# First norm and first projections of a two-layer decoder in an order written out for four engines, with identity turns ahead of the data

## The chip, the cores and the metric

The kernel runs on one core of a Trainium2 chip. The metric is the time of one execution on the device in microseconds (us), and the time given is the median of the runs. The core has TensorE (PE; its weight loads, PEld, are listed apart), VectorE (DVE), ScalarE (ACT), GpSimd (POOL) and the queue of SyncE (SPq), from which all transfers of this kernel are issued. TensorE writes its results into PSUM, eight banks of 512 fp32 columns, and reads both operands from SBUF.

## The reference

The kernel computes a two-layer decoder trunk over 1024 tokens of width 1024, in fp32. Only the beginning of the first layer matters here:

```python
def rms_norm(x, g):
    y = x * lax.rsqrt(jnp.mean(x * x, axis=-1, keepdims=True) + EPS)
    return y * g

def mla_swa_layer(x, positions, g_in, w_in, g_q_a, w_q_up, g_kv_a, w_kv_up, sinks, w_out):
    h = rms_norm(x, g_in)
    z = h @ w_in
    cq, ckv, kpe, q_s, k_s, v_s, gate = split_cols(z, EVEN_SPLITS)   # 256, 128, 32, 512, 128, 128, ...
    q = rms_norm(cq, g_q_a) @ w_q_up
    kv = rms_norm(ckv, g_kv_a) @ w_kv_up
    ...  # rotary on parts of q and on kpe, latent attention, window attention, gate, output projection
```

The second layer (forgetting attention) and the final norm follow.

## The kernel before

Every fp32 product is made of three matmuls: both operands are split into a rounded high part and a low part (high x high, low x high, high x low; `mm3`, lines 114 to 116). So each weight and each activation that TensorE reads has first been cast on ScalarE (the high part) and subtracted on VectorE or GpSimd (the low part): `split` (L105 and L106) for tiles that come out of PSUM, `split_sb` (L110 and L111) for weights in SBUF.

The tokens are 8 blocks of 128, handled as two halves of four blocks. For the first norm, each block's 1024 values are squared and summed (`square_sum`, L143 on VectorE, L146 on ScalarE), `inv_rms` (L118 to L139) makes 1/sqrt by a starting guess and three rounds of Newton's method on VectorE, and the row is multiplied by it (`row_norm`, L560 to L574, which deals the rows out to engines). `norm_T` (L200) then turns the half chunk by chunk: for each of the 8 chunks of 128 features, four 128x128 transposes into one PSUM bank (L206) and a split with the gain, which gives `hh` and `hl`.

The projections of a block of tokens (`token_project`) keep the activations stationary and stream the weights: 24 matmuls of 256 columns per block for the query latent (`za`, banks `pj`), 24 matmuls of 288 columns for the key/value latent, the rope key and the window values (`zb`, banks `s`). Each block has its own accumulator, filled over all 8 chunks before the next block begins. Then the latents are normed, turned and split again (`cT`), tables of cosines and sines are turned (`csE`, `csO`, L726 to L736), the rope keys are made (`krs`), the window keys are projected (`swa_k`), and the up-projections (`up_q`, `up_k`, `up_v`) begin.

A planner puts the instructions of each engine into an order by its own simulated times; the program text gives only the priorities. `tc.issue_after(ins)` keeps a group behind an instruction of the same engine, and inside `tc.manual_schedule(engines=...)` the named engines take their instructions in the order of the text. In the kernel before, only TensorE's order in the two attention parts is written out that way. The weights come through four buffers of 2 KB (`wr`), so a weight transfer waits until an older piece has been split.

Of the kernel before, what the change touches and what calls it, by code (L numbers as in the profile page):

```python
# [12 lines left out]
F32R = mybir.dt.float32r  # L13
# [5 lines left out]
P = 128  # L19
# [31 lines left out]
WORK0 = "q1 g0 q2 s0 q3 s1 s2 s3 a1 p0 b1 p1 g2 p2 g3 p3"  # L51
W_START0 = "FFFLLFLFLF"
# [7 lines left out]
def trunk(ctx, tc, x, positions, e_g_in, e_w_in, e_g_q_a, e_w_q_up, e_g_kv_a, e_w_kv_up,  # L60
# [13 lines left out]
            "wr": (4, 2048), "wh": (3, 2048), "wl": (3, 2048),  # L74
# [43 lines left out]
    def inv_rms(ssq, n, width, more=None):  # L118
# [13 lines left out]
        for _ in range(3):  # L132
            if n == 1:
                nc.vector.scalar_tensor_tensor(out=t, in0=y, scalar=y, in1=h, op0=ALU.mult, op1=ALU.mult)
            else:
                nc.vector.tensor_tensor(out=t, in0=y, in1=y, op=ALU.mult)
                nc.vector.tensor_tensor(out=t, in0=t, in1=h, op=ALU.mult)
            nc.vector.scalar_tensor_tensor(out=y, in0=t, scalar=1.5, in1=y, op0=ALU.add, op1=ALU.mult)
# [27 lines left out]
    def token_weights(pieces, cuts, tags_h, tags_l):  # L166

        n = sum(b - a for _, a, b in pieces)
        parts = []
        for (k0, kn), th, tl in zip(cuts, tags_h, tags_l):  # L170
# [7 lines left out]
            parts += [(wh[:, k, :], wl[:, k, :]) for k in range(kn)]  # L178
        return parts, n
# [20 lines left out]
    def norm_T(blocks, hT, gcol):  # L200

        hh, hl = hT
# [5 lines left out]
        return last  # L208
# [327 lines left out]
    nc.vector.tensor_copy(out=post, in_=p_ps[:, 0:NB])  # L536
    cost, sint = sbt("og", [NB, 16]), sbt("og", [NB, 16])
# [22 lines left out]
    def row_norm(rows, vector, groups, engines):  # L560
        ssq = sbt("sm", [4])
        for b in range(4):
            square_sum(rows[b], ssq[:, b:b + 1], vector[b] == "V")
        for a, n in groups:
            y = inv_rms(ssq[:, a:a + n], n, D)
            for b in range(a, a + n):
                yb = y[:, b - a:b - a + 1]
                if engines[b] == "A":
                    nc.scalar.activation(out=rows[b], in_=rows[b], func=AF.Copy, scale=yb)
                elif engines[b] == "P":  # L570
                    normalise(rows[b], yb, 1.0)
                else:
                    last = nc.vector.tensor_scalar(out=rows[b], in0=rows[b], scalar1=yb, scalar2=None, op0=ALU.mult)
        return last.ins  # L574
# [30 lines left out]
    g_ps = pst("pj", 32)  # L605
    nc.tensor.transpose(out=g_ps[:, 0:19], in_=gst[0:19], identity=ident[0:19, 0:19])
    gains = cp.tile([P, 19], F32, name="gains")
    nc.vector.tensor_copy(out=gains, in_=g_ps[:, 0:19])
# [13 lines left out]
    hT = []  # L622
    for hf in range(2):
        rows = xrows[4 * hf:4 * hf + 4]
        if hf:
            with tc.issue_after(normed):
                normed = row_norm(rows, "AAAV", [(0, 1), (1, 3)], "PVVA")
        hT.append(new_hT())
        made = norm_T([lambda k, r=r: r[:, k * P:(k + 1) * P] for r in rows], hT[hf], 0)

    with tc.issue_after(normed):
# [4 lines left out]
    with tc.issue_after(made):  # L636
        nc.vector.tensor_scalar(out=nsinks, in0=sinks, scalar1=-1.0, scalar2=None, op0=ALU.mult)


    zb, _ = token_weights([(w0, 256, 416), (w0, VS, VS + 128)], [(0, 3), (3, 3), (6, 2)],  # L640
                          ["kh", "kh", "kx"], ["kl", "kl", "kx"])
    kpe = sbt("gt", [NB, 32])
    cqs, ssq_q, ssq_kv = [], [], []
    for hf in range(2):
        cq, ssq = sbt("r1", [4, 256]), sbt("sm", [4])
        for b in range(4):
            acc = pst("pj", 256)
            token_project(hf * 4 + b, hT, za, acc)
            nc.vector.tensor_copy(out=cq[:, b, :], in_=acc)
            square_sum(cq[:, b, :], ssq[:, b:b + 1])  # L650
        cqs.append(cq)
        ssq_q.append(ssq)
# [24 lines left out]

    cT = [(sbt("qh", [S], F32R), sbt("ql", [S], F32R)) for _ in range(2)]
    for hf in range(2):
        y = inv_rms(ssq_q[hf], 4, 256)  # L680
        for b in range(4):
            nc.vector.tensor_scalar(out=cqs[hf][:, b, :], in0=cqs[hf][:, b, :], scalar1=y[:, b:b + 1],
                                    scalar2=None, op0=ALU.mult)
        for c in range(2):
            t = pst("t")
            for b in range(4):
                nc.tensor.transpose(out=t[:, b * P:(b + 1) * P], in_=cqs[hf][:, b, c * P:(c + 1) * P],
                                    identity=ident)
            cols = slice(hf * 512, (hf + 1) * 512)
            split(cT[c][0][:, cols], cT[c][1][:, cols], t, gains[:, 16 + c:17 + c])  # L690
    ckv = sbt("r1", [NB, P])
    for hf in range(2):
        ssq = sbt("sm", [4])
        for b in range(4):
# [99 lines left out]
    for _ in swa_k():  # L794
        pass
# [447 lines left out]
```

## Time and profile before

| what | us |
|---|---|
| median of 3 runs (1208.22 to 1209.9) | 1209.25 |
| profiled execution | 1211.98 |
| its span, first to last instruction | 1209.8 |
| TensorE busy in the span | 1164.8 (96%) |
| VectorE busy | 736.1 (61%) |
| ScalarE busy | 712.1 (59%) |
| GpSimd busy | 606.6 (50%) |

Times inside the kernel are counted from the start of the span. A busy time counts an engine's instructions from start to end. Matmuls are pipelined, so the step from one start to the next tells more of TensorE's speed than a duration does. The column for the granted TensorE clock is 1.00 in every stretch listed here.

### The profile page before, as it was taken

How to read it: one execution, taken by the hardware profiler on the slowest of the kernel's cores; microseconds unless marked ns; L12 is line 12 of the kernel's file. 1: busy time of each engine (PE TensorE's matmuls, PEld its weight loads, DVE VectorE, ACT ScalarE, POOL GpSimd, SP SyncE). 2: the span in 40 equal slices, each digit the busy share in tenths (PEclk: the TensorE clock that was granted, in tenths of full speed). 3: DMA queues.
4: the chain of work that ended last, by engine and by line, in shares of the span. 5: the costliest groups of instructions: out<-in, count | busy, mean ns of one | idle time of the engine just before them, and what ended most of it. 6: DMA issues, size and time to landing. Idle time of an engine off the chain costs nothing. (4 is left out here: it accounts for less than half of the span.)

```text
span 1209.8 us, 20486 instructions
## 1 busy us (share of the span) xinstructions
PE 1164.8 (96%) x6746; PEld 1010.1 (83%) x6746; DVE 736.1 (61%) x1962; ACT 712.1 (59%) x1599; POOL 606.6 (50%) x753
## 2 busy tenths in 40 slices
PE   4999999999898989999999999999999999999997
PEld 4997788888887878889998888888888888878886
DVE  8954466677676776665003666666656666657754
ACT  5634477776676765664214666676767666756442
POOL 6501144564765666433204555556565555568552
PEclk9999999999999999999999999999999999999999
DMA  6316412443755544563313221313131223236541
GB/s 213 91 43 231 152 45 69 119 139 103 204 149 144 166 139 153 171 212 105 114 44 107 62 79 58 92 53 88 53 94 62 83 69 102 65 122 212 185 161 61
DMA packets 171168, 139.52 MB, mean 115 GB/s; under 512 B 54027, under 2 KB 140838, under 8 KB 171062
## 3 DMA queue, kind: packets, MB, share of 16 engines
q1 hardware_dynamic: 171062, 138.21, 38.0%
q8 instruction: 53, 0.87, 0.3%
q14 instruction: 53, 0.43, 0.1%
HBM read 100.62 MB, written 37.55 MB: 114 GB/s over the span
## 5 line engine op out<-in xcount | busy, mean ns | idle before, releaser
L114 PE MATMUL pj<-hh,wh 128*128 128x512 f32 (+1 forms) x792 | 320.8, 405 | 2.2 <-ACT wh L110 0.9
L116 PE MATMUL pj<-hh,wl 128*128 128x512 f32 (+1 forms) x792 | 309.3, 391 | 0.6 <-POOL wl L111 0.6
L115 PE MATMUL pj<-hl,wh 128*128 128x512 f32 (+1 forms) x792 | 308.9, 390 | 0.0
L111 POOL TENSOR_TENSOR wl<-wr,wh 128x512 fp32r<-128x512 f32 (+1 forms) x146 | 183.8, 1261 | 161.6 <-ACT wh L110 153.4
L103 DVE TENSOR_TENSOR pl<-t,ph 128x512 fp32r<-128x512 f32 (+1 forms) x320 | 178.8, 563 | 86.6 <-ACT ph L102 84.3
L276 POOL TENSOR_SCALAR r<-r,sm 128x128 f32<-128x128 f32 (+4 forms) x248 | 167.1, 682 | 106.9 <-DVE sm L323 60.0
L102 ACT CAST ph<-t 128x512 fp32r<-128x512 f32 (+1 forms) x320 | 153.5, 483 | 106.4 <-PE t L347 86.0
L116 PEld LDWEIGHTS pj<-hh,wl 128*128 128x128 f32 x792 | 148.8, 188 | 33.5 <-POOL wl L111 1.1
L321 ACT ACTIVATE r<-r,sm 128x128 f32<-128x128 f32 (+7 forms) x184 | 143.0, 777 | 53.7 <-DVE sm L314 52.0
L114 PEld LDWEIGHTS pj<-hh,wh 128*128 128x128 f32 x792 | 149.3, 189 | 24.7 <-ACT wh L110 1.3
L115 PEld LDWEIGHTS pj<-hl,wh 128*128 128x128 f32 x792 | 149.6, 189 | 20.3
L347 PE MATMUL t<-ident,r 128*128 128x128 f32 x828 | 137.5, 275 | 11.6 <-DVE pl L103 9.1
L347 PEld LDWEIGHTS t<-ident,r 128*128 128x128 f32 x828 | 102.8, 141 | 40.0 <-DVE pl L103 11.2
L110 ACT CAST wh<-wr 128x512 fp32r<-128x512 f32 (+1 forms) x146 | 87.5, 600 | 58.1 <-PE pj L115 24.4
L308 POOL TENSOR_TENSOR ld<-ld,zrow 128x128 f32<-128x128 f32 x128 | 58.7, 468 | 99.7 <-DVE sm L314 80.2
L338 PE MATMUL o<-ph,v 128*128 128x512 f32 (+3 forms) x288 | 106.9, 371 | 0.0
L314 DVE CUSTOM_DVE_ANT_0 r<-s,ld 128x512 f32<-128x512 f32 (+1 forms) x120 | 70.5, 588 | 50.2 <-PE s L261 45.9
L339 PE MATMUL o<-pl,v 128*128 128x512 f32 (+3 forms) x288 | 99.4, 346 | 0.0
L285 POOL TENSOR_TENSOR v<-ge,v 128x512 fp32r<-128x512 f32 x26 | 34.6, 1330 | 71.1 <-ACT v L284 71.1
L338 PEld LDWEIGHTS o<-ph,v 128*128 128x128 f32 x288 | 54.9, 191 | 7.0
L339 PEld LDWEIGHTS o<-pl,v 128*128 128x128 f32 x288 | 54.6, 190 | 5.7
L114 PE MATMUL pj<-qh,hh 128*128 128x256 f32 (+1 forms) x176 | 50.9, 290 | 3.2 <-DVE gt L1057 1.7
(324 smaller groups left out, 2516.0 us busy)
## 6 DMA issues: line engine op xcount, KB each, us to landing
wr<-in_o_w_in SPq DMA_DIRECT2D x62, 256.0 KB, 3.1
wr<-ogs SPq DMA_DIRECT2D x44, 256.0 KB, 3.8
ld<-lcs SPq DMA_DIRECT2D x16, 512.0 KB, 4.1
ogs<-og SPq DMA_DIRECT2D x28, 256.0 KB, 2.0
ge<-vscr SPq DMA_DIRECT2D x24, 256.0 KB, 3.8
gt<-x1s SPq DMA_DIRECT2D x23, 256.0 KB, 2.9
wr<-ogs SPq DMA_DIRECT2D x24, 192.0 KB, 3.0
wr<-in_e_w_in SPq DMA_DIRECT2D x16, 256.0 KB, 3.3
```

Of the source, the lines that this page charges most:

```text
L102: nc.scalar.copy(out=hi, in_=src)
L103: nc.vector.tensor_tensor(out=lo, in0=src, in1=hi.bitcast(F32), op=ALU.subtract)
L110: nc.scalar.copy(out=hi, in_=raw)
L111: (engine or nc.gpsimd).tensor_tensor(out=lo, in0=raw, in1=hi.bitcast(F32), op=ALU.subtract)
L114: nc.tensor.matmul(out=o, lhsT=ah, rhs=bh, start=first, stop=False)
L115: nc.tensor.matmul(out=o, lhsT=ah, rhs=bl, start=False, stop=False)
L116: nc.tensor.matmul(out=o, lhsT=al, rhs=bh, start=False, stop=last)
L276: nc.gpsimd.tensor_scalar(out=row, in0=row, scalar1=rc, scalar2=scale, op0=ALU.mult, op1=ALU.mult)
L321: nc.scalar.activation(out=row[:, 0:L], in_=row[:, 0:L], func=AF.Exp, scale=-1.0, bias=mn, accum_out=den)
L338: nc.tensor.matmul(out=O[0][:, cols], lhsT=v()[:, j, :], rhs=ph[:, cols], start=j == 0, stop=False)
L339: nc.tensor.matmul(out=O[0][:, cols], lhsT=v()[:, j, :], rhs=pl[:, cols], start=False, stop=j == n - 1)
L347: nc.tensor.transpose(out=t[:, b * P:(b + 1) * P], in_=rows[b][:, j * P:(j + 1) * P], identity=ident)
```

## The change

Nothing is computed differently but for the form of three rounds in `inv_rms`. What moves or is added:

- 58 transposes of the identity into a bank that is not read (`WARM`), on TensorE ahead of the first data.
- For one value per partition, `inv_rms` uses `tensor_scalar` with two scalar operands in place of `scalar_tensor_tensor`.
- `wr` has six buffers; the first four weight pieces are loaded by name (`za_raw`).
- The first half's rows are squared, scaled and multiplied in a written order on four engines: row 0 squared on VectorE and rows 1 to 3 on ScalarE, one scale chain per row (`row_scales`), the products on GpSimd but for half of row 3.
- The query latent of a half is accumulated chunk by chunk in four banks at once (`latent_q`: two `pj`, two `o`): per chunk, twelve matmuls over the four blocks, two chunks behind the turns.
- Between these chunks the second half's rows are squared, at the seventh chunk their four scales are made together and the products written, and after it the second weight set is split.
- TensorE then takes, in a written order, the second half's turns between the first half's key/value blocks, the second half's query latent, and the other key/value blocks with the turns of the latents and the window keys among them.
- The rotary angles and the sinks' sign are issued behind the last split of the second half.

```diff
+WARM = 58
-            "wr": (4, 2048), ...
+            "wr": (6, 2048), ...
             if n == 1:
-                nc.vector.scalar_tensor_tensor(out=t, in0=y, scalar=y, in1=h, op0=ALU.mult, op1=ALU.mult)
...
+                nc.vector.tensor_scalar(out=t, in0=y, scalar1=y, scalar2=h, op0=ALU.mult, op1=ALU.mult)
+                nc.vector.tensor_scalar(out=y, in0=t, scalar1=1.5, scalar2=y, op0=ALU.add, op1=ALU.mult)
+                continue
...
+    idle = pst("o")
+    with tc.manual_schedule(engines={mybir.EngineType.PE}):
+        for j in range(WARM):
+            nc.tensor.transpose(out=idle[:, (j % 4) * P:(j % 4 + 1) * P], in_=ident, identity=ident)
...
-    normed = row_norm(xrows, "VVAA", [(0, 2), (2, 1), (3, 1)], "VAVV")
-    za, _ = token_weights([(w0, 0, 256)], [(0, 4), (4, 4)], ["qh", "qh"], ["ql", "ql"])
+    za_raw = []
+    for k in range(0, KC, 2):
+        raw = sbt("wr", [2, 256])
+        load_cols(raw, [(w0, 0, 256)], k, 2)
+        za_raw.append(raw)
...
+    def row_scales(ssqs):
+        rows = [tuple(sbt("sm", [1]) for _ in range(4)) for _ in ssqs]
+        for (a, h, y, t), ssq in zip(rows, ssqs):
+            nc.vector.tensor_scalar(out=a, in0=ssq, scalar1=1.0 / D, scalar2=EPS, op0=ALU.mult, op1=ALU.add)
+        for a, h, y, t in rows:
+            nc.vector.tensor_scalar(out=y.bitcast(I32), in0=a.bitcast(I32), scalar1=-0.5, ...)
+            nc.vector.tensor_scalar(out=h, in0=a, scalar1=-0.5, scalar2=None, op0=ALU.mult)
+        for _ in range(3):
+            for a, h, y, t in rows:
+                nc.vector.tensor_scalar(out=t, in0=y, scalar1=y, scalar2=h, op0=ALU.mult, op1=ALU.mult)
+            for a, h, y, t in rows:
+                nc.vector.tensor_scalar(out=y, in0=t, scalar1=1.5, scalar2=y, op0=ALU.add, op1=ALU.mult)
+        return [y for a, h, y, t in rows]
...
+    def latent_q(hf):
+        cq, ssq = sbt("r1", [4, 256]), sbt("sm", [4])
...
+        accs = [pst("pj" if b < 2 else "o", 256) for b in range(4)]
+        hh, hl = hT[hf]
+        for k in range(KC):
+            wh, wl = za[k]
+            for m, (h, w) in enumerate(((hh, wh), (hl, wh), (hh, wl))):
+                for b in range(4):
+                    nc.tensor.matmul(out=accs[b], lhsT=h[:, k, b * P:(b + 1) * P], rhs=w, start=k + m == 0,
+                                     stop=(k, m) == (KC - 1, 2))
+            if k < KC - 1:
+                yield
+        for b in range(4):
+            nc.vector.tensor_copy(out=cq[:, b, :], in_=accs[b])
+            square_sum(cq[:, b, :], ssq[:, b:b + 1])
+        yield
...
+    with tc.manual_schedule(engines={ET.PE, ET.DVE, ET.Activation, ET.Pool}):
+        ssq = [sbt("sm", [1]) for _ in range(NB)]
+        for b in range(4):
+            square_sum(xrows[b], ssq[b], b == 0)
+            y, = row_scales(ssq[b:b + 1])
+            if b < 3:
+                normalise(xrows[b], y, 1.0)
+            else:
+                last = nc.vector.tensor_scalar(out=xrows[b][:, 0:512], in0=xrows[b][:, 0:512], scalar1=y, ...)
+                normalise(xrows[b][:, 512:D], y, 1.0)
...
+        for k in range(0, KC, 4):
+            wh, wl = sbt("qh", [4, 256], F32R), sbt("ql", [4, 256], F32R)
+            za += [(wh[:, i, :], wl[:, i, :]) for i in range(4)]
+            for i in (0, 2):
+                split_sb(wh[:, i:i + 2, :], wl[:, i:i + 2, :], za_raw[(k + i) // 2])
+
+        turns, steps = first_norm(0), None
+        for k in range(KC + 2):
+            made = next(turns, None) or made
+            if k == 1:
+                steps = latent_q(0)
+            if k > 1:
+                next(steps)
+            if 1 < k < 6:
+                b = k + 2
+                square_sum(xrows[b], ssq[b], b == 6)
+            if k == 6:
+                ys = row_scales(ssq[4:])
+                normalise(xrows[4], ys[0], 1.0)
+                normalise(xrows[5], ys[1], 1.0)
+                nc.vector.tensor_scalar(out=xrows[6], in0=xrows[6], scalar1=ys[2], scalar2=None, op0=ALU.mult)
+                nc.scalar.activation(out=xrows[7], in_=xrows[7], func=AF.Copy, scale=ys[3])
+            if k > 6:
+                for _ in range(3):
+                    next(zb_steps, None)
+    kpe = sbt("gt", [NB, 32])
+    with tc.manual_schedule(engines={ET.PE}):
+        turns = first_norm(1)
+        for b in range(4):
+            for _ in range(2):
+                made = next(turns, None) or made
+            latent_kv(b)
+        for _ in latent_q(1):
+            pass
+        latent_kv(4)
+        turn_cq(0)
+        latent_kv(5)
+        turn_ckv(0)
+        latent_kv(6)
+        turn_cq(1)
+        latent_kv(7)
+        for _ in swa_k():
+            pass
+        turn_ckv(1)
+    with tc.issue_after(made):
         rotary(sint, 0.0)
         rotary(cost, 0.25)
+        nc.vector.tensor_scalar(out=nsinks, in0=sinks, scalar1=-1.0, scalar2=None, op0=ALU.mult)
```

`latent_kv(blk)` is the 24 matmuls of one block with `zb` into a `pj` bank and the copies out of it; `turn_cq` and `turn_ckv` are the norms, turns and splits of the latents; `zb_steps` loads and splits the second weight set one chunk per step (eight steps). All three hold what the removed code held.

## Rows read from the trace of the kernel before

**Rows 1.** Windows: busy us (x instructions) per engine, clock, DMA share, GB/s.

```profile
20.00:40.00 20.00, 19.44 (x151) 19.17 (x151) 19.38 (x50) 15.67 (x43) 10.50 (x17) 1.00 0.34 94
40.00:60.00 20.00, 19.16 (x155) 18.92 (x154) 17.48 (x56) 12.17 (x41) 13.19 (x25) 1.00 0.33 79
...
80.00:100.00 20.00, 18.62 (x106) 15.76 (x105) 15.23 (x45) 10.18 (x22) 3.82 (x3) 1.00 0.33 85
```

**Rows 2.** Timeline of TensorE: start us, duration us, engine, line, operation, tiles.

```profile
19.55 0.58 PE L114 MATMUL pj<-qh,hh 128*128 128x256 f32 x1
...
22.06 0.41 PE L116 MATMUL pj<-qh,hl 128*128 128x256 f32 x1
22.27 0.41 PE L114 MATMUL pj<-qh,hh 128*128 128x256 f32 x1
...
23.81 0.28 PE L114 MATMUL pj<-qh,hh 128*128 128x256 f32 x1
23.93 0.28 PE L115 MATMUL pj<-ql,hh 128*128 128x256 f32 x1
...
43.21 0.30 PE L114 MATMUL s<-kh,hh 128*128 128x288 f32 x1
43.34 0.29 PE L115 MATMUL s<-kl,hh 128*128 128x288 f32 x1
...
88.56 1.04 PE L735 MATMUL s<-ident,r 128*128 128x128 f32 x8
```

**Rows 3.** Groups on TensorE up to 43.21 us: count | busy us, mean ns | idle before.

```profile
L114 PE MATMUL pj<-qh,hh 128*128 128x256 f32 x44 | 13.2, 302 | 0.7 <-DVE r L649 0.6
L115 PE MATMUL pj<-ql,hh 128*128 128x256 f32 x44 | 12.9, 297 | 0.0
L116 PE MATMUL pj<-qh,hl 128*128 128x256 f32 x42 | 12.8, 315 | 0.0
```

**Rows 4.** Timeline of VectorE: the first rows, a latent norm, the last scale.

```profile
4.59 1.32 DVE L143 CUSTOM_DVE_ANT_0 ge<-r 128x1024 bf16<-128x1024 f32 x1 [1.24 <-DMA r<-in_x]
...
10.95 0.15 DVE L123 TENSOR_SCALAR sm<-sm 128x1 f32<-128x1 f32 x1
11.02 1.17 DVE L134 SCALAR_TENSOR_TENSOR sm<-sm,sm 128x1 f32<-128x1 f32 x1
...
17.48 0.75 DVE L573 TENSOR_SCALAR r<-r,sm 128x1024 f32<-128x1024 f32 x1
18.15 0.15 DVE L123 TENSOR_SCALAR sm<-sm 128x1 f32<-128x1 f32 x1
...
18.58 0.22 DVE L134 SCALAR_TENSOR_TENSOR sm<-sm,sm 128x1 f32<-128x1 f32 x1
...
74.16 0.88 DVE L712 TENSOR_SCALAR r<-r,sm 128x128 f32<-128x128 f32 x4
...
1203.85 0.21 DVE L125 TENSOR_SCALAR sm<-sm,sm 128x1 f32<-128x1 f32 x1
1204.10 0.22 DVE L134 SCALAR_TENSOR_TENSOR sm<-sm,sm 128x1 f32<-128x1 f32 x1
...
1205.52 0.49 DVE L1211 TENSOR_SCALAR r<-r,sm 128x512 f32<-128x512 f32 x1
```

**Rows 5.** Timeline of GpSimd: a weight's low part, a row's product, four low parts.

```profile
10.81 1.35 POOL L111 TENSOR_TENSOR ql<-wr,qh 128x512 fp32r<-128x512 f32 x1 [0.90 <-ACT qh L110]
...
21.75 1.12 POOL L276 TENSOR_SCALAR ld<-ld,sm 128x1024 f32<-128x1024 f32 x1 [5.21 <-ACT hh L105]
24.87 3.10 POOL L111 TENSOR_TENSOR kl<-wr,kh 128x288 fp32r<-128x288 f32 x4 [2.01 <-ACT kh L110]
```

**Rows 6.** Groups on ScalarE and VectorE up to 110 us, columns as in rows 3.

```profile
L106 DVE SCALAR_TENSOR_TENSOR hl<-s,gains,hh 128x512 fp32r<-128x512 f32 x8 | 5.9, 742 | 0.7 <-ACT hh L105 0.5
...
L105 ACT ACTIVATE hh<-s,gains 128x512 fp32r<-128x512 f32 x8 | 5.5, 688 | 3.8 <-PE s L206 3.8
...
L569 ACT ACTIVATE kx<-kx,sm 128x1024 f32<-128x1024 f32 x1 | 1.1, 1148 | 0.0
```

More of the change, by code (lines that the diff above doesn't have):

```diff
@@ new lines, in latent_kv @@
+    def latent_kv(blk):
+        b = blk % 4
+        if blk == 0:
+            ckv.append(sbt("r1", [NB, P]))
+        if b == 0:
+            ssq_kv.append(sbt("sm", [4]))
+        acc = pst("pj", 288)
+        token_project(blk, hT, zb, acc)
+        nc.vector.tensor_copy(out=ckv[0][:, blk, :], in_=acc[:, 0:P])
+        nc.vector.tensor_copy(out=kpe[:, blk, :], in_=acc[:, P:P + 32])
+        square_sum(ckv[0][:, blk, :], ssq_kv[-1][:, b:b + 1])
+        vst = sbt("ob", [P])
+        nc.scalar.copy(out=vst, in_=acc[:, 160:288])
+        nc.sync.dma_start(out=vscrs[blk * P:(blk + 1) * P], in_=vst)
@@ new lines, in trunk, with turn_cq @@
+    cT = []
+    def turn_cq(hf):
+        y = inv_rms(ssq_q[hf], 4, 256)
+        for b in range(4):
+            nc.vector.tensor_scalar(out=cqs[hf][:, b, :], in0=cqs[hf][:, b, :], scalar1=y[:, b:b + 1],
+                                    scalar2=None, op0=ALU.mult)
+        for c in range(2):
+            if hf == 0:
+                cT.append((sbt("qh", [S], F32R), sbt("ql", [S], F32R)))
+            t = pst("t")
+            for b in range(4):
+                nc.tensor.transpose(out=t[:, b * P:(b + 1) * P], in_=cqs[hf][:, b, c * P:(c + 1) * P],
+                                    identity=ident)
+            cols = slice(hf * 512, (hf + 1) * 512)
+            split(cT[c][0][:, cols], cT[c][1][:, cols], t, gains[:, 16 + c:17 + c])
@@ new lines, in turn_ckv @@
+    def turn_ckv(hf):
+        if hf == 0:
+            cT.append((sbt("v", [S], F32R), sbt("v", [S], F32R)))
+        y = inv_rms(ssq_kv[hf], 4, 128)
+        t = pst("t")
+        for b in range(4):
+            blk = hf * 4 + b
+            nc.vector.tensor_scalar(out=ckv[0][:, blk, :], in0=ckv[0][:, blk, :], scalar1=y[:, b:b + 1],
+                                    scalar2=None, op0=ALU.mult)
+            nc.tensor.transpose(out=t[:, b * P:(b + 1) * P], in_=ckv[0][:, blk, :], identity=ident)
+        cols = slice(hf * 512, (hf + 1) * 512)
+        split(cT[2][0][:, cols], cT[2][1][:, cols], t, gains[:, 18:19])
@@ new lines, in trunk, with swa_k @@
+    swa = {}
+    def swa_k():
+        swa["k"] = sbt("kh", [S], F32R), sbt("kl", [S], F32R)
+        swa["kx"] = new_kx()
+        yield from project([(w0, KS, KS + P)], hT, stack_k(*swa["k"], swa["kx"]))
+    ET = mybir.EngineType
+    with tc.manual_schedule(engines={ET.PE, ET.DVE, ET.Activation, ET.Pool}):
+        ssq = [sbt("sm", [1]) for _ in range(NB)]
+        for b in range(4):
+            square_sum(xrows[b], ssq[b], b == 0)
[3 more added lines that the diff above has]
+            else:
+                last = nc.vector.tensor_scalar(out=xrows[b][:, 0:512], in0=xrows[b][:, 0:512], scalar1=y,
+                                               scalar2=None, op0=ALU.mult)
+                normalise(xrows[b][:, 512:D], y, 1.0)
+        g_ps = pst("pj", 32)
+        nc.tensor.transpose(out=g_ps[:, 0:19], in_=gst[0:19], identity=ident[0:19, 0:19])
+        nc.vector.tensor_copy(out=gains, in_=g_ps[:, 0:19])
+        for k in range(0, KC, 4):
[22 more added lines that the diff above has]
+                    next(zb_steps, None)
@@ L642, in trunk @@
[L642 to L652, printed above, removed]
     wq = []
@@ L1016, in next_norm @@
         hT_next.append(new_hT())
-        norm_T(parts, hT_next[hf], 8)
+        for _ in norm_T(parts, hT_next[hf], 8):
+            pass
     def out0(nh, blk):
```

107 lines of the change are left out of this document (24 added, 83 removed).

## The prediction

> **What bounds the kernel now.** I read the busy time of each engine in stretches of 20 us first: from 20 us on TensorE is busy nearly all the time, and what it is idle in the stretches to 100 us adds up to 0.56 + 0.84 + 1.38 us [rows 1]. So the kernel is a stream of TensorE work, and a change at its head is worth what it takes from TensorE's *lost* time there, as long as no other engine takes the place. Then I read TensorE's list in order of time, for the step from one instruction to the next of the same form. A projection matmul of 256 columns steps by 0.21 us at 22.06 and by 0.12 us at 23.81: 256 columns are 1.2 GHz in the first case and 2.4 GHz (nearly) in the second, although the column for the granted clock prints 1.00 in both stretches. A turn (a 128-column transpose) steps by 0.11 us at the higher level (eight in 1.04 us, of which the last is 0.27) and a 288-column matmul by 0.13 us [rows 2]. Third, the groups of TensorE instructions up to 43.21 us: 44 + 44 + 42 = 130 matmuls of 256 columns [rows 3], and all 64 turns of the first norm are by then behind them in the program.
>
> This gives a ledger. At 43.21 us TensorE has done 130 x 0.12 + 64 x 0.11 = 22.6 us of work at the higher level, so 20.6 us are lost: waiting for the first rows, single turns between waits, some 4 us at half speed (the first matmul is at 19.55 [rows 2]), 0.56 us for an accumulator. With the 0.84 and the 1.38 us that follow, the kernel before has lost **22.8 us by 100 us**. The same sum for the changed kernel decides.
>
> **The change part by part: up to the first projection.** Rows 0 to 3 have to be squared, scaled and multiplied before a chunk can be turned. The first square ends at 4.59 + 1.32 = 5.91 [rows 4]. Then the written order puts four scale chains one behind the other on VectorE, as each is called with one row. A chain is 0.43 us up to its first operation with a pointer scalar (18.15 to 18.58) and then six operations on one element, each needing the one before. These are now `tensor_scalar` with pointers. The nearest row is a `tensor_scalar` with one pointer, whose follower begins 0.25 us later (1203.85 to 1204.10) [rows 4]. A chain is 0.43 + 6 x 0.25 = 1.93 us, four are 7.7 us, so the last scale is there at 13.7. The squares on ScalarE are shorter than the chains and fall beside them, and rows 0 to 2 are multiplied on GpSimd (1.12 us each [rows 5]) beside the next chain. Half of row 3 goes on VectorE: a whole row is 0.75 us [rows 4], a half about 0.42, so the first full chunk is turned from **14.2 us**. The operation with two pointers has no row. If the second pointer costs again what the first does (0.135 against 0.07 us in the spacing, below), each chain is 0.2 us longer; if pointers cost nothing in this form, a step is 0.19 us and a chain 1.57. I take one pointer's price.
>
> What the new form does remove is the stall behind GpSimd: at 11.02 a `scalar_tensor_tensor` on one element took 1.17 us while GpSimd ran its 1.35 us subtraction from 10.81, and the `tensor_scalar` at 10.95 inside the same subtraction took 0.15 [rows 4, 5]. With immediates, that is; with pointers no row shows it.
>
> **The projection by chunks.** A chunk is four turns and twelve matmuls: 0.44 + 1.44 = 1.88 us. Its split costs 0.69 us on ScalarE and 0.74 us on VectorE [rows 6], so TensorE sets the pace. Three chunks are turned ahead (to 15.5), the first latent chunk waits some 0.2 us for its low part and ends at 17.2, and the seventh chunk is turned at 17.2 + 3 x 1.88 + 0.44 = 23.3. The weights' low parts (four of about 1.3 us on GpSimd, from 14.8 [rows 5]) are there in time. If nothing stopped it the projection of the first half would end at 29.5.
>
> **What stops it.** Behind the seventh split (23.3 + 0.69 + 0.74 and a handover: 24.8) VectorE has the scales of rows 4 to 7 in one run: 36 operations, 12 with immediates at 0.07 us of spacing (10.95 to 11.02) and 24 with pointers. Four pointer operations on 128 elements take 0.88 us, 0.22 each; at the pace of a whole row (0.75 us for 1024) the 128 elements are 0.09 of that, and about 0.135 remain for an operation on one element [rows 4]. 12 x 0.07 + 24 x 0.135 = 4.1 us, to 28.9. Three engines wait in line for that. ScalarE has row 7's product (1.15 us [rows 6]) written ahead of the eighth chunk's high part, so the last latent chunk, which would have begun at 28.1, begins at 31 and ends at 32.4. GpSimd multiplies rows 4 and 5 (2 x 1.12 us, with VectorE's row 6, 0.75 us, between them, since the two keep each other out as at 11.02): 31.6. Only behind these come the low parts of the second weight set, eight of 3.10 / 4 = 0.78 us [rows 5]: 37.8. TensorE turns two chunks of the second half (to 33.3) and then stands in the first latent/value block, whose eighth chunk needs the eighth low part: it ends at **38.3** instead of 36.5. By then the work is 40 turns, 96 matmuls of 0.12 and 24 of 0.133: 19.1 us. Lost: **19.2 us**, of which 5 are this new wait.
>
> **The rest.** The third latent block of the first half and the second half's projection share two banks, so TensorE waits twice for a copy, as it does for 0.56 and 0.84 us in the kernel before [rows 1]: I take 0.9. The 1.38 us between 80 and 100 us [rows 1] stand where cosines, rope keys and the first up-projections meet; they may stay or go (0 to 1.38), and as the turned tables still come right ahead of the up-projection I take 0.7. Work on the DMA queue keeps its order up to 13 us; two more `wr` buffers let two loads go ahead, and the last two weight pieces wait for low parts that GpSimd frees at 32.4 and 33.2: hidden as long as they land by 36. At the end of the kernel one chain of the new form lies on the path: six operations took 1204.10 to 1205.52, and 6 x 0.25 is 0.1 us more [rows 4]. The 58 identity turns cost nothing if they are done by 14.2: from about 2.75 us they need 58 x 0.11 = 6.4 us at the higher level (9.1) and 58 x 0.21 = 12.2 us at the lower (15).
>
> Sum: 19.2 + 0.9 + 0.7 + 0.1 = 20.9 us lost against 22.8, a gain of **1.9 us**. The profiled execution took 1211.98 us (span 1209.8 and 2.2 around it), so such a one becomes 1210.1; the median of the runs, 2.7 us below the profiled one, becomes 1207.4.
>
> **A rule that speaks against it.** The trace shows that turns run at the higher level once it is there (0.11 us [rows 2]); no row of before shows turns alone bringing it. The Trainium skill, "TensorE: Matmul & The Clock Gate", Part 4 (PE-mode transpose), says that transposes do not count as busy to the clock gate, so the full clock does not engage for them. By that rule the 58 turns stay at the lower level and warm nothing: that is the first rival.
>
> **The rivals.**
> *The clock is low at the first chunk.* Either the turns do not raise it, or it falls again between 9 and 14 us, when TensorE has single turns only. The turns then hold TensorE to 15 (0.9 us late), and the first 4 us of work go at half speed as they do now (1.9 us): 1207.4 + 2.8 = 1210.2, the gain gone. For it: the kernel before is still at the lower level at 22.06, after scattered turns and then matmuls. Against: those turns were few.
> *The scales are cheap.* If pointers cost nothing in this form, four chains end 1.4 us earlier and the run of 36 takes 2.5 us instead of 4.1; all that hangs on them moves: a gain of about 2.7 more, 1204.7. For it: the immediate form beside it steps by 0.07. Against: the pointer rows.
> *Slower: the run of 36 does not overlap.* If each operation waits for the one before as in a single chain, it is 36 x 0.25 = 9.0 us instead of 4.1, at one place, ahead of rows 4 to 7, with ScalarE, GpSimd and TensorE queued behind: 1207.4 + 4.9 = 1212.3. It ends above the time before once an operation costs over 0.17 us on average. Against: 0.07 and 0.135 us of spacing between operations that don't need each other.
> *The second pointer* (0.2 us a chain, 0.7 us in the run: 1.4 us in all, 1208.8) is a bound of the forecast, no case of its own.
>
> **How the numbers follow.** Forecast 0.42 (1207.4, by itself 1205.5 to 1209.5), low clock 0.25 (1210.2), cheap scales 0.20 (1204.7), no overlap 0.13 (1212.3). Some 0.2%, 2.4 us, is what can be told from no change. Below 1206.8: cheap scales 0.19 and 0.14 of the forecast, 0.33. Above 1211.7: no overlap 0.12 and 0.06 of the low clock, 0.18. Between: 0.49. The engines' order behind the edited part may shift and has no row; I allow it 1 us inside these cases. The range, 1204.0 to 1211.8, leaves about one in ten out at either end.
>
> **What would show it.** Right: the first four-turn chunk near 14.2 us; matmul steps of 0.12 us from the first latent chunk on; TensorE idle before the last latent chunk (29 to 31) and inside the first 288-column block, waiting for GpSimd's low parts. Wrong: steps of 0.21 us there (low clock); VectorE's run of 36 well below or above 4.1 us; no wait in the first 288-column block; or idle time of more than 1 us that is new behind 40 us.

## The result and the profile after

The changed kernel takes **1222.07 us** (median; 1217.63 to 1223.02), the kernel before beside it 1209.58 us: a ratio of **1.0101**, 95% interval [1.0087, 1.0115]. It is 12.5 us slower where 1.9 us of gain were forecast; the time lies outside the range. The profiled execution took 1222.22 us (span 1220.4). Ratios here and below compare runs on the same chip and leave disturbed runs out, so they don't always agree with the quotient of two medians.

The loss is complete within the first 140 us. The copies of the query up-projection (the product with the sines and cosines, line 860, 771 before) are 16; the last begins at 127.7 us before and at 140.2 us after, 12.5 us later, while the end of the span moves by 10.6 us (before, then after):

```profile
127.66 0.69 DVE L771 TENSOR_TENSOR r<-pj,r 128x512 f32<-128x512 f32 x1 [0.67 <-PE pj L116]
140.16 0.69 DVE L860 TENSOR_TENSOR r<-pj,r 128x512 f32<-128x512 f32 x1 [0.67 <-PE pj L117]
```

This last copy is the milestone of all that follows. Up to it TensorE carries out the same 686 instructions in both kernels and in each of the twelve kernels below, identity turns apart, so it compares equal work. What lies behind it took 1076.0 to 1082.3 us in the fourteen profiled executions, before and after alike (1082.1 and 1080.2). So the rest of this document looks at the head. The windows that answer [rows 1], kernel after:

```profile
20.00:40.00 20.00, 16.76 (x122) 16.19 (x121) 13.52 (x50) 10.72 (x22) 7.75 (x9) 0.90 0.24 60
40.00:60.00 20.00, 16.69 (x113) 15.78 (x111) 7.28 (x17) 9.10 (x27) 8.66 (x10) 0.91 0.29 85
...
80.00:100.00 20.00, 18.38 (x116) 17.31 (x117) 14.09 (x72) 5.28 (x15) 0.00 (x0) 0.91 0.08 21
```

TensorE (first busy figure) stands still for 3.2, 3.3 and 1.6 us of these stretches, where it was 0.56, 0.84 and 1.38 before. That is one half. The other half is the number behind the busy times: the granted clock is 0.90 and 0.91, where [rows 1] have 1.00. Finer windows, TensorE alone (length, busy us and instructions, clock, DMA share, GB/s):

```profile
15.00:20.00 5.00, 4.91 (x23) 0.50 0.75 246
30.00:34.00 4.00, 1.33 (x10) 1.00 0.01 2
34.00:38.00 4.00, 4.00 (x19) 0.57 0.27 66
40.00:44.00 4.00, 2.44 (x15) 1.00 0.53 161
44.00:48.00 4.00, 4.00 (x20) 0.57 0.67 206
58.00:61.00 3.00, 0.52 (x5) 1.00 0.42 87
61.00:65.00 4.00, 4.00 (x23) 0.57 0.44 95
78.00:82.00 4.00, 1.39 (x10) 0.99 0.06 18
82.00:85.00 3.00, 3.00 (x14) 0.50 0.02 5
20.00:100.00 80.00, 70.10 (x484) 0.91 0.24 62
```

They come in pairs: a window in which TensorE mostly waits, and behind it one in which it is fully busy at half clock (0.50 is 1.2 GHz). Four times a wait is paid a second time so, and once ahead of them, from 13.7 to 20.5 us. TensorE's timeline shows both, the waits in brackets and the two speeds as the step between pairs of matmuls (0.24 us at 60.95 to 61.19, 0.42 at 61.82 to 62.24):

```profile
1.42 4.96 PE L549 MATMUL o<-ident 128*128 128x128 f32 x22 [1.42 <-POOL ident masks.py:199]
...
6.50 4.29 PE L549 MATMUL o<-ident 128*128 128x128 f32 x36
...
17.93 0.63 PE L659 MATMUL pj<-qh,hl 128*128 128x256 f32 x2
18.36 0.63 PE L659 MATMUL o<-qh,hl 128*128 128x256 f32 x2
...
20.34 0.55 PE L659 MATMUL pj<-qh,hh 128*128 128x256 f32 x2
...
33.10 0.33 PE L214 MATMUL s<-ident,ld 128*128 128x128 f32 x1 [2.10 <-POOL ld L284]
34.00 0.70 PE L659 MATMUL pj<-qh,hh 128*128 128x256 f32 x2 [0.57 <-ACT hh L106]
...
42.14 0.40 PE L115 MATMUL pj<-kx,hh 128*128 128x288 f32 x1 [0.91 <-ACT kx L111]
43.10 0.40 PE L116 MATMUL pj<-kx,hh 128*128 128x288 f32 x1 [0.56 <-POOL kx L112]
...
60.73 0.38 PE L659 MATMUL pj<-qh,hh 128*128 128x256 f32 x1 [2.48 <-ACT ob L680]
60.95 0.40 PE L659 MATMUL o<-qh,hh 128*128 128x256 f32 x2
61.19 0.40 PE L659 MATMUL pj<-qh,hl 128*128 128x256 f32 x2
...
61.82 0.63 PE L659 MATMUL pj<-ql,hh 128*128 128x256 f32 x2
62.24 0.63 PE L659 MATMUL o<-ql,hh 128*128 128x256 f32 x2
...
79.14 0.66 PE L829 MATMUL s<-ident,r 128*128 128x128 f32 x4 [0.79 <-DVE r L830]
81.62 2.12 PE L695 MATMUL t<-ident,r 128*128 128x128 f32 x8 [1.82 <-DVE r L688]
```

What the waits wait for stands on three engines. VectorE, in order of time: the run of 36 scale operations begins at 27.68 and ends at 32.0 us, and row 6's product follows; near 58 us the sines and cosines (lines 555 and 562) run ahead of the copies of the fourth latent/value block (line 676), which ScalarE's square and its own copy out of the same bank follow (line 680, the one that the wait at 60.73 names):

```profile
27.68 0.33 DVE L630 TENSOR_SCALAR sm<-sm 128x1 f32<-128x1 f32 x4
...
32.04 1.55 DVE L756 TENSOR_SCALAR kx<-kx,sm 128x1024 f32<-128x1024 f32 x1
...
58.16 0.92 DVE L555 TENSOR_SCALAR ph<-gt 128x128 f32<-128x128 f32 x1
59.00 0.76 DVE L562 COPY gt<-gt 128x128 f32<-128x128 f32 x1
...
59.75 0.28 DVE L676 COPY r<-pj 128x128 f32<-128x128 f32 x1
...
62.87 0.36 DVE L555 TENSOR_SCALAR ph<-gt 128x128 f32<-128x128 f32 x1
```

GpSimd (the products of rows 4 and 5, six of the eight low parts, and a weight's low parts that lie beside VectorE's slow operations at 58 and 59 us), then ScalarE (row 7's product ahead of the eighth chunk's high part, the last two casts of the second weight set, and the copy of line 680):

```profile
31.93 2.64 POOL L284 TENSOR_SCALAR ld<-ld,sm 128x1024 f32<-128x1024 f32 x2 [11.39 <-DVE sm L639]
34.54 4.59 POOL L112 TENSOR_TENSOR kl<-wr,kh 128x288 fp32r<-128x288 f32 x6
...
56.88 2.79 POOL L112 TENSOR_TENSOR ld<-wr,ld 128x256 fp32r<-128x256 f32 x4
```

```profile
32.22 1.15 ACT L757 ACTIVATE kx<-kx,sm 128x1024 f32<-128x1024 f32 x1 [5.24 <-DVE sm L639]
33.28 0.67 ACT L106 ACTIVATE hh<-t,gains 128x512 fp32r<-128x512 f32 x1
...
41.67 0.75 ACT L111 CAST kx<-wr 128x288 fp32r<-128x288 f32 x2
...
60.43 0.25 ACT L680 COPY ob<-pj 128x128 f32<-128x128 f32 x1
```

### The profile page after: what moved, and what is told of

Its sections match the earlier page's. It is cut to its first block, busy times and chain, and to the rows that moved or that the text cites. A ratio compares the mean times of both kernels' runs of the same rounds, so it can differ in the third digit from the quotient of the medians.

```text
span 1220.4 us, 20628 instructions
## 1 busy us (share of the span) xinstructions
PE 1181.2 (97%) x6804; PEld 1027.0 (84%) x6804; DVE 726.1 (59%) x1978; ACT 712.0 (58%) x1600; POOL 611.3 (50%) x758
## 5 line engine op out<-in xcount | busy, mean ns | idle before, releaser
L284 POOL TENSOR_SCALAR r<-r,sm 128x1024 f32<-128x1024 f32 (+4 forms) x252 | 171.4, 688 | 111.9 <-DVE sm L331 67.1
L116 PEld LDWEIGHTS pj<-hl,wh 128*128 128x128 f32 x792 | 150.1, 190 | 20.5
L148 ACT ACTIVATE ge<-r 128x512 bf16<-128x512 f32 (+3 forms) x44 | 24.2, 551 | 55.1 <-DVE r L1085 23.8
```

The costliest lines, as they stand in the source:

```text
L116: nc.tensor.matmul(out=o, lhsT=ah, rhs=bl, start=False, stop=False)
L284: nc.gpsimd.tensor_scalar(out=row, in0=row, scalar1=rc, scalar2=scale, op0=ALU.mult, op1=ALU.mult)
```

## The theory and the table that tests it

**Theory A:** the changed order makes TensorE wait in more and longer places than the order before, and most of these waits make the clock fall for the next stretch too; the 12.5 us are the two together. **Rival B:** the waits alone count, and the clock would have fallen anyway. **Rival C:** only one of the two written blocks is to blame. And beside these: the 58 identity turns bought nothing (A) or something.

One row of the windows carries the test for each kernel: 20 to 100 us, TensorE's busy time and clock. For the kernel before it is

```profile
20.00:100.00 80.00, 77.22 (x549) 1.00 0.29 74
```

80 - 77.22 = 2.8 us idle and nothing lost to the clock by the column, though its steps of 0.21 us at 22.06 [rows 2] say that the lower level lasts to some 23 us and takes about 1.5 us there (half of the 3.00 us that it is busy from 20 to 23). For the changed kernel 80 - 70.10 = 9.9 us idle and (1 - 0.91) x 80 = 7.2 us lost at half speed: 17.1 us. That is 17.1 - 4.3 = 12.8 us worse. At 20 us the changed kernel is 8 instructions ahead (28 against 20, identity turns apart), about 1 us, so the row makes 11.8 us of the 12.5 at the milestone. The same row for all kernels, with the milestone and the time. "Turns" are identity turns inside 20 to 100 us, at 0.11 us each: they count as busy in the row and as idle here. "Gaps" are the waits between the four turns of the first chunk, and e1 to e12 the experiments below. The first three columns come from one profiled execution each, whose time lies up to 4.6 us from the median beside it.

| kernel | idle + turns | lost to the clock | last copy of the query up-projection | median us | ratio to before, 95% |
|---|---|---|---|---|---|
| before | 2.8 | 0 (1.5 by its steps) | 127.7 | 1209.6 | 1 |
| changed | 9.9 | 7.2 | 140.2 | 1222.1 | 1.0101 [1.0087, 1.0115] |
| one wait filled (e1) | 7.5 + 2.4 | 4.8 | 140.7 | 1218.4 | 1.0076 [1.0052, 1.0099] |
| all waits filled (e2) | 1.8 + 8.5 | 0 | 131.8 | 1214.1 | 1.0038 [1.0021, 1.0055] |
| no turns (e3) | 11.1 | 8.8 | 140.9 | 1220.2 | 1.0080 [1.0051, 1.0109] |
| before, with 58 turns (e4) | 3.8 | 1.6 | 128.3 | 1212.9 | 1.0017 [0.9999, 1.0035] |
| second block to the planner (e5) | 4.3 | 2.4 | 128.6 | 1211.0 | 1.0009 [0.9993, 1.0026] |
| first block reordered (e6) | 5.1 | 1.6 | 128.0 | 1210.3 | 1.0015 [1.0004, 1.0027] |
| VectorE's two moves (e7) | 7.4 | 3.2 | 134.8 | 1216.4 | 1.0053 [1.0036, 1.0070] |
| both orders moved, gaps filled (e8) | 2.2 | 0 | 122.8 | 1204.0 | 0.9960 [0.9943, 0.9976] |
| the same, gaps open (e9) | 2.4 | 0 | 123.5 | 1205.5 | 0.9964 [0.9944, 0.9984] |
| the same, no turns (e10) | 2.4 | 0 | 124.0 | 1207.4 | 0.9978 [0.9965, 0.9991] |
| first block reordered, second to the planner, gaps filled (e11) | 0 | 0 | 119.5 | 1199.5 | 0.9922 [0.9903, 0.9940] |
| three more moves (e12) | 3.1 | 1.6 | 125.6 | 1205.1 | 0.9967 [0.9954, 0.9980] |

## The experiments

### Fill the waits, take none away

Identity turns into PSUM columns that nothing reads before they are written anew stand where TensorE waits; every wait of the computation stays. First in one place, the 2.48 us at 60.7 us:

```diff
                     nc.tensor.matmul(out=accs[b], lhsT=h[:, k, b * P:(b + 1) * P], rhs=w, start=k + m == 0,
                                      stop=(k, m) == (KC - 1, 2))
+                    if hf and k + m + b == 0:
+                        idle_turns(22, accs[2][:, 0:P])
```

> The changed kernel with one addition: 22 identity turns (2.4 us at 0.11 each) into an accumulator bank not yet in use, behind the first matmul of the second half's query projection, where TensorE waits 2.48 us for the copies of the fourth latent/value block. Nothing else moves. Theory A (a wait of TensorE costs its length and, behind it, a stretch at the lower clock): the granted clock of the stretch behind 61.4 us goes from 0.50 to 1.00, the wait itself is as long, and the milestones from 70 us on come 1.7 us earlier: about 1220.4 us (1222.1 - 1.7), ratio to the kernel before about 1.0087. Rival B (the lower clock there has nothing to do with the wait): the stretch stays at 0.50 and the time at 1222.1, ratio 1.010.

The stretch behind it is at full clock:

```profile
58.00:61.00 3.00, 2.92 (x26) 1.00 0.40 87
61.00:65.00 4.00, 4.00 (x36) 1.00 0.48 102
```

At the first copy of the query up-projection 1.5 us are there (108.3 us against 109.8), of which 0.3 stood ahead of the filled wait already. Behind that the profiled run gives them back: the last copy comes at 140.7 against 140.2, with 1.1 us more idle time between 84 and 156 us (waits of 0.69 and 0.30 us for copies by ScalarE that the changed kernel didn't have) and about 1 us that no row explains. The median is 3.7 us lower, and so is the profiled span, but not by what the head gained: behind the milestone the changed kernel's trace has 3.4 us more of lower clock (380 to 400 and 440 to 460 us), and the intervals of the two overlap. The row of the clock carries this experiment, the time alone would not.

Then in all of the larger waits up to 84 us: the one just filled and, in the order of the diff, the first half's `norm_T` (gaps of 8, 17 and 9), `latent_q`, the first latent/value block (5 more inside its seventh chunk) and `turn_cq`:

```diff
+    def idle_turns(n, to):
+        for _ in range(n):
+            nc.tensor.transpose(out=to, in_=ident, identity=ident)
...
+                if gaps and k == 0 and b < 3:
+                    idle_turns(gaps[b], idle[:, 0:P])
...
+            if hf == 0 and k == KC - 1:
+                idle_turns(20, pst("t", P))
...
+            if pad is not None and k == 6:
+                idle_turns(10, pad)
...
+            if hf + c == 0:
+                idle_turns(20, t[:, 0:P])
```

> The changed kernel with identity turns in all of its larger TensorE waits up to 84 us: 8, 17 and 9 between the four turns of the first chunk, 20 ahead of the last latent chunk of the first half, 10 + 5 in the first latent/value block, 22 in the second half's query projection, 20 ahead of the turns of the first half's latents. No wait of the computation is removed. Theory A (the loss is the waits plus the lower clock behind them): the five stretches at the lower level (13.7 to 20.5, 34.2 to 37.6, 44.4 to 47.8, 61.5 to 64.9, 81.9 to 85.3) go, which is up to 9.5 us; the waits stay at about 10 us. I expect 1214 us (1212.5 to 1216.5), ratio 1.004. Rival B (the waits and the written order alone made the loss): 1222, no change, however the clock stands.

```profile
15.00:20.00 5.00, 4.96 (x40) 1.00 0.85 295
...
20.00:100.00 80.00, 78.25 (x587) 1.00 0.28 71
```

1214.1 us, the forecast of theory A to 0.1 us: none of the five stretches is left, 77 turns between 20 and 100 us are work that nobody needs, and the kernel is still 8 us faster. Rival B, which sees no gain here, falls. What stays, 4.5 us over the kernel before, goes with the waits, which are all still there (1.8 us idle and 8.5 us of turns in this stretch).

### The turns ahead of the data

```diff
-    idle = pst("o")
-    with tc.manual_schedule(engines={mybir.EngineType.PE}):
-        for j in range(WARM):
-            nc.tensor.transpose(out=idle[:, (j % 4) * P:(j % 4 + 1) * P], in_=ident, identity=ident)
```

> The changed kernel without the 58 identity turns ahead of the first data. Theory A: they bought nothing, since the clock had fallen again at 13.7 us, before the first chunk: same time, 1222 us (within 1.2), the first matmuls at 0.21 us a step with and without. Rival (the turns gave some of the clock back, or held TensorE up): 1.5 to 2 us slower without them, or about 1 us faster.

1220.2 us, 1.9 below the changed kernel and a little more than the 1.2 that was allowed for, with an interval that holds its 1.0101: no difference that can be told. In the trace the turns even cost a little: without them the second latent chunk starts at 19.54 us, with them at 20.34 (above), as the clock comes up earlier there.

```profile
19.54 0.48 PE L655 MATMUL pj<-qh,hh 128*128 128x256 f32 x2
```

The same four lines added to the kernel before, ahead of its sines and cosines:

> The kernel before with the 58 identity turns alone added ahead of its first data. Theory A: the clock rises at about 6.8 us and falls again in the gaps ahead of the first matmul at 19.55, so nothing changes: 1209.6 us (within 1). Rival (a warm start holds): the matmuls from 19.55 on step by 0.12 instead of 0.21 us up to 23.5, worth 1.7 to 1.9 us: 1207.8.

No gain, rather a small loss (1212.9 us, ratio 1.0017, the interval just reaches 1). The higher clock comes with the turns and is gone again when the work begins: the first rows' turns at 13 us step by 0.11 us, those behind a wait of 4.17 us by 0.21.

```profile
13.21 0.27 PE L206 MATMUL t<-ident,r 128*128 128x128 f32 x1
13.32 0.27 PE L206 MATMUL s<-ident,r 128*128 128x128 f32 x1
...
18.14 0.42 PE L206 MATMUL t<-ident,r 128*128 128x128 f32 x1
18.35 0.42 PE L206 MATMUL s<-ident,r 128*128 128x128 f32 x1
```

### Which block

```diff
     kpe = sbt("gt", [NB, 32])
-    with tc.manual_schedule(engines={ET.PE}):
-        turns = first_norm(1)
...
+    turns = first_norm(1)
...
```

> The changed kernel with the second written block undone: the statements of the second half's turns, latents and keys stay in the changed kernel's sequence, but TensorE's order there is the planner's again. The first block stays as written. Theory A: the waits of the second block (2.48 at 60.7, 0.79 + 1.82 at 79 to 82) belong to its written order, and with them go the two lower-clock stretches behind them: 5.1 + 2 x 1.7 = 8.5 us, of which the planner's own waits (1 to 3 us, as 0.84 + 1.38 in the kernel before) come back: 1215 to 1217 us. Rival B (all of it comes from the first block): 1221 to 1222.

1211.0 us, 4 us below the lower end of what was expected:

```profile
20.00:100.00 80.00, 75.69 (x535) 0.97 0.31 76
```

5.6 us less idle time and 4.8 us less lost to the clock than in the changed kernel; the 0.91 and 0.56 us of the first latent/value block, which I had put down to the first block, went as well, since the planner puts other work there: the next block's matmuls, more turns and the first of the second half's projection.

The other way round, the first block with its orders moved and nothing added:

```diff
-            if k == 6:
-                ys = row_scales(ssq[4:])
+            if k == 3:
+                ys = row_scales(ssq[4:6])
                 normalise(xrows[4], ys[0], 1.0)
                 normalise(xrows[5], ys[1], 1.0)
-                nc.vector.tensor_scalar(out=xrows[6], in0=xrows[6], scalar1=ys[2], scalar2=None, op0=ALU.mult)
-                nc.scalar.activation(out=xrows[7], in_=xrows[7], func=AF.Copy, scale=ys[3])
-            if k > 6:
-                for _ in range(3):
-                    next(zb_steps, None)
+            if k == 6:
+                ys = row_scales(ssq[6:])
+            if k == 7:
+                nc.vector.tensor_scalar(out=xrows[6], in0=xrows[6], scalar1=ys[0], scalar2=None, op0=ALU.mult)
+                nc.scalar.activation(out=xrows[7], in_=xrows[7], func=AF.Copy, scale=ys[1])
+            for _ in range({4: 2, 6: 2, 7: 1, 8: 3}.get(k, 0)):
+                next(zb_steps, None)
```

> The changed kernel with the first block's order altered and no work added: the scales of rows 4 and 5 with their products move from the seventh chunk to the fourth, those of rows 6 and 7 stay behind the seventh, the products of rows 6 and 7 move behind the eighth chunk's split, and the eight steps of the second weight set go in from the fifth chunk on instead of behind the eighth. This takes away the waits 2.10 and 0.57 (33 to 34 us) and 0.91 + 0.56 (42 to 43 us). Theory A: 4.1 us of waits and two stretches at the lower clock, 2 x 1.7: 7.5 us less, 1214.6 us (1213 to 1217). Rival B (waits cost their own length only): 4.1 us less, 1218. Rival C (given back later, at the second block): 1221 to 1222.

1210.3 us: the waits at 33, 34, 42 and 43 us are gone (4.7 us with the 0.57 at 38.6), and with them the clock's stretches behind them; 4 us more than forecast again. Of these, 1.4 come ahead of 20 us, where the edit changes nothing: the first stretch at half clock happens to be half as long (a clock of 0.91 instead of 0.84 up to 20 us). Another 1.7 lie behind a wait that stayed. The wait of 2.49 us for the fourth block's copies is still there, only earlier, and this time the clock does **not** fall behind it:

```profile
50.12 0.39 PE L659 MATMUL pj<-qh,hh 128*128 128x256 f32 x1 [2.49 <-ACT ob L680]
```

```profile
50.00:60.00 10.00, 9.88 (x82) 1.00 0.42 90
```

So the clock's part of a wait isn't a fixed price. The changed kernel's own six runs differ too: the one with a mean clock of 0.992 took 1217.6 us, the one with 0.985 took 1222.2 (where in the kernel these two differ is not on record). Rival C falls with these two experiments: either block alone, mended, brings back most of the loss, 11.0 and 11.8 us. By the table about half of each gain came through the clock (4.8 and 5.6 us), so the two don't add up: behind some of the waits that stayed the clock did not fall.

The second block mended in another way, on VectorE alone: `copied` is the fourth latent/value block's last copy, and `scale_cq`, the scales and products at the head of `turn_cq`, stands for the first half at the end of the first written block.

```diff
-    with tc.issue_after(made):
+    with tc.issue_after(copied):
         rotary(sint, 0.0)
...
+        scale_cq(0)
     kpe = sbt("gt", [NB, 32])
```

> The changed kernel with two things moved on VectorE and no work added: the sines and cosines are held back until the copies of the fourth latent/value block (as things are they run ahead of them), and the scales and products of the first half's query latents are issued at the end of the first written block instead of ahead of their turns at 81 us. This takes away about 1.9 of the 2.48 us at 60.7 and the 1.82 at 81.6. Theory A: 3.7 us of waits and up to two lower-clock stretches, 2 x 1.7: 5.4 to 7.1 us less, 1215 to 1217 us. Rival B (waits cost their own length only): 3.7 less, 1218.4.

1216.4 us, as theory A forecast (5.4 to 7.1 less; measured 5.7). The wait at 60.7 us is 0.91 instead of 2.48, the one at 81.6 is 0.5, and the clock holds behind both.

### Together, and below the kernel before

The two diffs above in one kernel, and the gaps of the first chunk filled:

```diff
+                          None if hf else (8, 17, 9))
```

> The two kernels of moved orders together, and identity turns (8, 17, 9) between the four turns of the first chunk, so that the clock holds from the first turns on. Theory A: the three parts add up, 7.5 + 5.4 to 7.1 + 2.7 us: 1222.1 - 16.5 = 1205.6 us (1203.5 to 1208), which is below the kernel before (1209.6). Rival B: 4.1 + 3.7 and nothing from the clock, 1214.

1204.0 us, 0.40% below the kernel before; 1205.6 was forecast. The row of 20 to 100 us: 77.80 busy at 1.00. Then the turns were taken back from it in two steps, first this last line, then also the 58:

> The kernel of moved orders (e8_best1) without the 8, 17 and 9 identity turns between the four turns of the first chunk; the 58 ahead of the first data stay. Theory A: the clock falls in the waits between the four turns, as in the changed kernel, and the first matmuls step by 0.21 us again up to about 20 us: 1.7 to 2.7 us slower than e8_best1's 1204.0, 1206 to 1207. Rival (58 turns are enough, or the start does not matter): 1204.

> The kernel of moved orders without any identity turn, neither the 58 nor those between the first chunk's turns. Theory A: as e9_best_nogaps, 1206 to 1207, since the 58 alone buy nothing; the head then starts cold as in the kernel before. Rival (the 58 alone buy some of the clock): another 1 to 2 us slower, 1208.

1205.5 and 1207.4 us. The intervals overlap; the milestone, free of the later clock, says 122.8, 123.5, 124.0 (one execution each). By it turns in the gaps are worth 0.8 us and the 58 another 0.5: less than forecast, as the clock comes up by 17.5 us without the gaps' turns and by 18.4 us without any, instead of 20.5.

Next the first block reordered with its gaps filled, and the second block without `manual_schedule` (the diffs of both stand above):

> The first written block with moved orders (e6_order1) and turns between the first chunk's four, and the second block left to the planner (e5_planner2). Theory A, block by block: first block 4.7 us of waits and 3.4 of clock, second block 5.1 us of waits less 1.5 of the planner's own and 3.4 of clock, first chunk 2.7: 1222.1 - 17.8 = 1204.3 (1203 to 1207). If the gains of e5_planner2 and e6_order1, 11.0 and 11.8 us, were each wholly of its own block: 1222.1 - 22.8 - 2.7 = 1196.6.

**1199.5 us, 0.78% below the kernel before** and the best of all. TensorE has no idle time and no lower clock in 80 us:

```profile
20.00:100.00 80.00, 80.00 (x561) 1.00 0.41 114
```

The planner starts the second half's query projection in the two banks that are free while the fourth block's copies are under way, which the written order of the second block can't. The sum by blocks (1204.3) was 5 us too high, the full gains added (1196.6) 3 us too low.

And three more moves in the kernel of 1204.0 us (with 68 turns ahead and 9, 7 and 3 in the gaps), of which the two that answer in the trace are

```diff
-            y, = row_scales(ssq[b:b + 1])
...
+        for a in (0, 2):
+            for b, y in zip((a, a + 1), row_scales(ssq[a:a + 2])):
...
-        accs = [pst("pj" if b < 2 else "o", 256) for b in range(4)]
+        accs = [pst("pj" if (b < 2) == (hf == 0) else "o", 256) for b in range(4)]
```

> e8_best1 with three more moves: the scales of rows 0 to 3 in two pairs instead of four single chains (last scale near 12.5 instead of 14.5 us; rows 2 and 3 halved between VectorE and GpSimd, first chunk complete near 13.5 instead of 15.1), each latent/value block's last part copied ahead of its squares, and the second half's query projection begun in the two banks that are free (the 1.34 us wait at 48.1 us goes). 1.6 + 1.3 us less than e8_best1's 1204.0: 1201 (1200 to 1203). If the head is not what sets the end: 1204.

A miss: 1205.1 us, no better than 1204.0. Both targets were met (the fourth turn of the first chunk at 14.4 instead of 15.1 us, the wait of 1.34 us at 48 us gone), but the banks that the second half's projection now takes last are those that the fifth latent/value block needs first: in the profiled run, the slowest of the ten, a new wait of 1.45 us and behind it half clock again.

```profile
61.06 0.61 PE L115 MATMUL pj<-kh,hh 128*128 128x288 f32 x1 [1.45 <-DVE r L674]
```

```profile
61.00:65.00 4.00, 3.94 (x19) 0.60 0.29 72
```

## Why the prediction was wrong, point by point

**The method held, a term was missing.** The ledger of TensorE's lost time was the right account: the table repeats it from one row, and the milestone follows it. The step that failed is the ledger of the changed kernel, "19.2 + 0.9 + 0.7 + 0.1": it holds what TensorE waits and nothing for the clock behind a wait, and its waits are too short. It never asked what a wait does to the clock behind it, although its first rival was about just that, at the first chunk alone.

**The first block, 38.3 us forecast, 44.2 measured** (end of the first latent/value block: its last matmul starts at 44.10 us, the next instruction at 44.23). The mechanism was right in each step: VectorE's run of 36 took 4.36 us (27.68 to 32.04, where row 6's product begins; 4.1 forecast, so the rival "does not overlap", 9.0, and "cheap scales", 2.5, are both out), row 7's product stood ahead of the eighth chunk's high part, GpSimd took rows 4 and 5 and then low parts of 0.77 us. Three sizes were missed, 2.9 + 1.7 + 1.5 = 6.1 us against the 5.9 measured: the run began 2.9 us late, as the first chunk's last turn came at 15.1 instead of 14.2 (the first square ended at 6.3 instead of 5.9, and a chain is 2.0 us, not 1.93) and the work behind it ran at half speed up to 20.5; the last latent chunk ran at half clock (1.7 us); and the last two weight pieces were cast at 41.67 us, behind the squares of the latents that the written order puts first (0.91 + 0.56 us of wait; the prediction had them hidden "as long as they land by 36").

**"A warm start": the first rival came true.** It had a chance of 0.25. The turns did raise the clock (step 4.96 / 22 = 0.23 us, then 4.29 / 36 = 0.12; they ended by 10.8 us), it fell in the waits between the first chunk's four turns, and the first matmuls went at 0.21 us each (a pair from 17.93 to 18.36). It was priced at 2.8 us, and without the turns the kernel is no slower.

**The two bank hand-overs, 0.9 us forecast, 2.48 + 0.57 measured.** The prediction took two rows of before for them. In the changed kernel the sines and cosines had been moved behind the second half's last chunk, which is just ahead of the fourth block's copies on VectorE, and they were slow there: 0.92 us for an operation that takes 0.36 at 62.87. ScalarE's copy, which TensorE waited for, came behind all of it. The prediction moved them past TensorE's queue in thought, but not past VectorE's.

**The stretch of 80 to 100 us, 0.7 forecast, 0.79 + 1.82 measured.** The first half's latents were scaled only at 81 us, when their turns stood next in the written order. I had left out who scales them and when.

**The clock behind the waits, 0 forecast.** Behind the first block 3 x 1.7 = 5.1 us (44 to 48, 61 to 65, 82 to 85 us). With the first block's 5.9, 2.48 + 0.57 - 0.9 = 2.2 for the hand-overs, of which the 0.57 at 38.6 is already in the 5.9 (so 1.6), and 0.79 + 1.82 - 0.7 = 1.9 the misses come to 14.5 us; the milestone, forecast 22.8 - 20.8 = 2.0 us earlier (the 0.1 is at the end of the kernel, where the chain took 1.74 us instead of 1.42), missed its forecast by 12.5 + 2.0 = 14.5.

**Its own warnings.** "Idle time of more than 1 us that is new behind 40 us" was named as what would show it wrong, and stands at 60.7 and 81.6 us. Of its signs of being right, the wait inside the first 288-column block and the idle time ahead of the last latent chunk came (at 42 and at 31 to 34 us), the steps of 0.12 us from the first latent chunk on did not. The slower side was given 0.18: 0.12 to a mechanism that did not occur, 0.06 to the low clock at the first chunk.

## What to carry to other kernels

Price a wait of TensorE twice: by its length, and by the work behind it at half clock, which here came to almost three quarters as much again (7.2 us of clock to 9.9 of waits). Ahead of a written order, list for each step what stands before it on every engine's queue, copies out of PSUM above all: the best kernel let the planner put other work where a bank wasn't free, and its TensorE lost nothing in the same 80 us. Turns ahead of the data bought nothing here, where waits of 0.66 to 1.65 us came behind them; turns inside the waits bought 8 us.

## What the hardware showed that was not expected

Turns alone raise the clock: 22 identity turns step by 0.23 us on average and the next 36 by 0.12. The Trainium skill, "TensorE: Matmul & The Clock Gate", Part 4 (PE-mode transpose), says that the full clock doesn't engage for transposes. This trace disagrees for the turns of this kernel (`nc.tensor.transpose`, fp32), and in the kernel with all waits filled, turns and nothing else held the clock at 1.00 through every wait that they filled.

Short waits are enough for the clock to fall: 0.91 and 0.56 us within 1 us of each other ahead of 44.4 us, 0.79 and 1.82 ahead of 81.9. The Trainium skill, "TensorE: Matmul & The Clock Gate", section "A second HAM failure mode: psum-queue depth-cycling", tells of a clock that swings because TensorE idles briefly and often between groups of matmuls. This trace agrees as far as these two places go. But a single wait of 2.49 us at 47.6 to 50.1 left the clock alone in one kernel (first block reordered), and one of 2.48 us at 58.2 to 60.7 brought it down in another (changed), so the length alone does not decide. What tells the two apart was not tried.

A `tensor_scalar` on one element with two pointer scalars takes 0.27 us, and its follower begins 0.30 us later; the one with a pointer and an immediate 0.25. And VectorE's 128-column operations of lines 555 and 562 took 0.92 and 0.76 us beside GpSimd's low parts of 256 columns (56.88 us), 0.36 and 0.27 beside those of 128 columns (62.87 and 63.41 us), and 0.22 and 0.23 with GpSimd standing still (kernel with VectorE's two moves, 64.34 us), though neither is of the kind that stalled for 1.17 us in [rows 4].
